# Up projection of a gated MLP: two parts of x moved as 512 columns through one weight load, their products added by ScalarE and VectorE

## The chip, the cores and the metric

One NeuronCore of a Trainium2 chip. The metric is the device time of one execution in microseconds, the median of several runs. Engines are named as in the profile: PE (TensorE, with PEld for its weight loads), DVE (VectorE), ACT (ScalarE), POOL (GpSimd) and SP (SyncE, which issues the loads here).

## The reference

One layer of a decoder trunk on x of 256 rows and 1024 columns, float32. A combined input projection feeds attention, a short convolution and a pooling mixer; an output projection, a residual and a LayerNorm follow. The gated MLP is the part that the change touches:

```python
up = causal_dwconv(x @ w_up, ffn_conv_w) + ffn_conv_b   # w_up: 1024 x 5632, width-3 conv over rows
u, g = jnp.split(up, 2, axis=-1)                        # 2816 columns each
ff = (u * jax.nn.silu(g)) @ w_down                      # w_down: 2816 x 1024
return layer_norm(DEEPNORM_ALPHA * x + ff, ln2_g, ln2_b)
```

## The kernel before

Float32 products are made on TensorE from operands of type float32r. Each operand is split into two such parts whose sum it is: `split` (L120) has ACT round the tile to the first part, `hi` (L121), and DVE subtract that from the tile, which is the second part, `lo` (L122). Three products of the four are kept: `mm3` (L148, its matmul is L150) issues first part by first part, first weight part by second x part, and second weight part by first x part, into one PSUM sum. The parts of x are held in two tiles, `xh` and `xl`, as [128, 8 row tiles of the model dimension, 256 rows of x]. In the MLP the weight part is the operand that is loaded and x is the one that is moved: every matmul of the up projection has 128x128 weights and 256 columns.

Weights come from memory in loads of 128x2048 (SP, `load`, L94, five held), and are split by halves, called units, of 128x1024 (`wsplit`, L128, nine held). For the up projection a unit is one column tile of 128 output columns: `("u", j)` for the value half and `("g", j)` for the gate half, j from 0 to 21. A unit `("d", k)` is one row tile of w_down.

The work of one column tile j is:

- `up_mm(j, 0)` and `up_mm(j, 1)` (L437): 8 row tiles by 3 matmuls each. Both halves of a tile share one PSUM bank, `u_ps[j]`, 256 columns each. Tile 0 is made by `up_first` from unsplit operands and is not touched by the change.
- `taps(j, s)` (L457): the convolution over rows. ACT writes y = scale * src + bias from PSUM (L462), then DVE adds the two shifted products with multiply-adds (L463, L464), which read PSUM and y.
- `gate_silu(j)` (L466, ACT, L468) and `gate_out(j)` (L470): DVE multiplies the halves into f (L472), and f is split into mh (ACT, L121) and ml (DVE, L122).
- `down(k, t, p)` (L477): the down projection of row tile k, five column tiles later (LAG = 5), for two groups of 128 rows of x (t) and the pieces p of 512, 512 and 512, 256, 256 output columns. Its sums, `acc2`, take five of the eight PSUM banks from the first down block on. For the last seven row tiles (KEEP = 7) the second group's products come at the very end.

The order is written out by hand, and the program keeps it: every engine runs its instructions in the order in which they are emitted. The work is a list of blocks of matmuls: u of tile j, g of tile j, and from tile 5 on the down block of row tile j - 5. The loop at L638 emits a block's matmuls, then what follows the block before it (the taps), then the weight splits for blocks up to six ahead, then the gate of a finished tile. So from tile 6 on DVE's queue for a tile is: ml of the last tile, lo of a split, L463 and L464 of the value half, lo, L463 and L464 of the gate half, lo, f. ACT's is: mh, hi, y, hi, y, hi, silu. Tiles 1 to 5 have two splits in their time instead of three. PSUM banks come from a pool of eight, small tiles (y, silu, f) from a pool of 12 slots (`tmp`, L68).

The end of the kernel is `resid` and `ln2_out`: residual, LayerNorm and the store.

Of the kernel before, what the change touches and what calls it, by code (L numbers as in the profile page):

```python
# [17 lines left out]
P = 128  # L18
# [10 lines left out]
ALPHA = 2.0 ** 0.25  # L29
EPS = 1e-5  # L30
NEG = -1e30
H = 1024                # columns of a unit of weights, half of a load
RB = 5                  # loads held
WB = 9                  # split units held
AHEAD = (4, 7)          # blocks of matmuls that the splits may run ahead, before and from w_out on
LAG = 5                 # column tiles between the up and the down projection
KEEP = 7                # row tiles of w_down that the second token tile takes last
FIRST = 2               # row tiles of w_out that both token tiles take first
WARM = 23
# output columns of each token tile by the bank they are summed in: (first, number)  # L40
PIECES = (((0, 512), (512, 512)), ((0, 512), (512, 256), (768, 256)))

C_ID = 0
# [12 lines left out]
def trunk(ctx, tc, a_qk, a_v, a_cp, a_out, a_up, a_down, x, par, tab, lnp, out):  # L56
# [8 lines left out]
    def bank():  # L65
        return ps.tile([P, 512], F32, name="bank")

    def tmp(name):  # L68
        return wk.tile([P, S], F32, name=name, tag="t", bufs=12)

    # ---- weights: loaded in the order of use, and split by halves into two float32r parts
    # whose sum they are
    units = [("qk", k) for k in range(KD)]
    units += [(n, i) for n, c in (("v", 4), ("cp", KD), ("out", KD)) for i in range(c)]
    for j in range(NJ):
# [16 lines left out]
    raws, left = [], {}  # L92

    def load():  # L94
        # as far as the slots are free
        while len(raws) < len(loads) and (len(raws) < RB or not left[raws[len(raws) - RB]]):
            at, c = loads[len(raws)]
            key = id(at), c
            n = S + H if at is a_qk else 2 * H
            raw = raw_of[key] = rp.tile([P, n], F32, name="raw")  # L100
            if raws:
                nc.sync.dma_start(raw, at[c])
            else:
                nc.sync.dma_start(raw[:, :2 * S], at[c][:, :2 * S])
                nc.sync.dma_start(raw[:, 2 * S:], at[c][:, 2 * S:])
            raws.append(key)
            left[key] = 1 if at is a_qk else 2
# [43 lines left out]
                             skip_group_check=skip)  # L151

    tb = cp.tile([NB + 1, GW + NH], F32, name="tb")
    xh = cp.tile([P, KD, S], F32R, name="xh")
    xl = cp.tile([P, KD, S], F32R, name="xl")
    # the tensor engine's clock rises with use: some products of zeros while the first loads run
    zero = cp.tile([P, P], BF16, name="zero")
    nc.vector.memset(zero, 0.0)
    g_ps = warm = bank()
# [6 lines left out]
    attn = ExitStack()  # L166
    ap = attn.enter_context(tc.tile_pool(name="ap", bufs=1))

    # ---- relative bias, times 8, as bias[q reversed, k] for the second token tile
    bias = ap.tile([P, NH, S], F32, name="bias")  # L170

    def bias_mm():
# [8 lines left out]
            bias, bass.AP(tensor=g_dr.tensor, offset=g_dr.offset, ap=[[1, P], [GW, NH], [1, S]]))  # L181
        nc.gpsimd.dma_start(prm, par)

    # ---- q, k: one sweep over the model dimension, eight column tiles at once
    qk_ps = [bank() for _ in range(4)]

    def qk_block(k):
        h, l = W.pop(("qk", k))
        for c in range(8):
            ws = slice(c * P, (c + 1) * P)  # L190
            if k == 0 and c < 2:
                # the first two column tiles come before their splits
                raw = raw_of[id(a_qk), 0]
                nc.tensor.matmul(qk_ps[0][:, c * S:(c + 1) * S], raw[:, S + c * P:S + (c + 1) * P],  # L194
                                 raw[:, :S], start=c == 0, stop=False, skip_group_check=True)
                continue
            mm3(qk_ps[c // 2][:, (c % 2) * S:(c % 2 + 1) * S], h[:, ws], l[:, ws],
                xh[:, k, :], xl[:, k, :], k == 0 and c % 2 == 0, k == KD - 1, skip=True)
# [11 lines left out]
    s_ps, prs = {}, {}  # L210

    def scores(j):
        # two heads on the two halves of the rows, side by side
        pair = [(h, slice((h % 2) * DH, (h % 2 + 1) * DH)) for h in (2 * j, 2 * j + 1)]
        for h, _ in pair:
            s_ps[h] = bank()
        for h, r in pair:
            nc.tensor.matmul(s_ps[h][:, :P], qT[r, j, 0], kT[r, j, :P], start=True, stop=True)
        for h, r in pair:
            nc.tensor.matmul(s_ps[h][:, P:P + S], qT[r, j, 1], kT[r, j], start=True, stop=True)  # L220
# [43 lines left out]
        nc.vector.tensor_copy(hi, rev)  # L264
        nc.vector.tensor_sub(ml[:, j].rearrange("p (t q) -> p t q", t=NT), rev, hi.bitcast(F32))

    # ---- v
    v = ap.tile([P, NT, 512], F32, name="v")
    v_ps = []

# [12 lines left out]
        for t in range(NT):  # L283
            nc.scalar.activation(v[:, t], v_ps[t], AF.Copy)

    # ---- pool and conv columns: P0 P1 | CC0 CX0 | CB0 CC1 | CX1 CB1
    cps = {}

    def cp_block(i):
# [8 lines left out]

    def pool_sums(t, p_ps):
        p_ps = p_ps[:, :S]  # L300
        # window sums by doubling; the two halves of the partitions have their own windows
        p, a, b, d = tmp("pin"), tmp("pa"), tmp("pb"), tmp("pd")
        nc.scalar.activation(p, p_ps, AF.Copy)

        def step(dst, src, w, rows):
            nc.gpsimd.tensor_add(dst[rows, w:], src[rows, w:], src[rows, :S - w])
            nc.gpsimd.tensor_copy(dst[rows, :w], src[rows, :w])

        al, up = slice(0, P), slice(DH, P)
        step(a, p, 1, al)  # L310
        if t == 0:
            step(b, a, 2, up)
        else:
            step(b, a, 2, al)
            step(a, b, 4, al)
            step(b, a, 8, up)
        iw = prm[:, C_IW + t:C_IW + t + 1]
        ed = prm[:, C_ED + 16 * t:C_ED + 16 * t + 16]
        for rows, src in ((slice(0, DH), a), (up, b)):
            nc.gpsimd.tensor_mul(d[rows, :16], src[rows, :16], ed[rows])  # L320
            nc.gpsimd.tensor_scalar(d[rows, 16:], src[rows, 16:], iw[rows], None, op0=ALU.mult)
        nc.gpsimd.tensor_sub(d, d, p)
        return d
# [22 lines left out]
        nc.vector.tensor_mul(o, cb_ps[:, :S], y)  # L346
        to_mix(4 + t, o)

    # ---- residual stream and LayerNorm
    def ln_rows(i):  # L350
        t = fp.tile([P, 2, D], F32, name="lnp")
        for r in range(2):
# [2 lines left out]
        gb.append(t)  # L355

    def resid(t, c, n, acc):
        # alpha * x + acc of n columns from c on, and their statistics
        nc.vector.scalar_tensor_tensor(xr[:, t, c:c + n], xr[:, t, c:c + n], ALPHA, acc,
                                       op0=ALU.mult, op1=ALU.add)  # L360
        for q in range(c // S, (c + n) // S):
            nc.vector.bn_stats(stats[t][:, q], xr[:, t, q * S:(q + 1) * S])  # L362

    def norm_stats(t):
        # mean, variance, 1 / deviation
        mv = wk.tile([P, 3], F32, name="mv")
        nc.vector.bn_aggr(mv[:, :2], stats[t])
        nc.vector.tensor_scalar(mv[:, 2:], mv[:, 1:2], EPS, None, op0=ALU.add)  # L368
        nc.gpsimd.tensor_tensor(mv[:, 2:], mv[:, 2:], half, op=ALU.pow)  # L369
        return mv  # L370

    # ---- output projection; row tiles in the order 0 1 2 3 6 7 4 5
    order = (0, 1, 2, 3, 6, 7, 4, 5)
    acc = [[], []]

# [35 lines left out]
            nc.tensor.transpose(t_ps[t, hf][:, i * P:(i + 1) * P], xr[:, t, k * P:(k + 1) * P], ident)  # L411

    def ln1_cols(t, hf):
        # gain and offset on the transposed rows
        ts = slice(t * P, (t + 1) * P)
        for i in range(4):
            k = 4 * hf + i
# [12 lines left out]
        nc.gpsimd.tensor_mul(xr[:, t], xr[:, t], gb[0][:, 0])  # L430
        nc.gpsimd.tensor_add(xr[:, t], xr[:, t], gb[0][:, 1])

    # ---- gated MLP
    acc2 = [[], []]
    gt = {}

    def up_mm(j, s):  # L437
        h, l = W.pop(("ug"[s], j))
        if s == 0:
            u_ps[j] = bank()  # L440
        for k in range(KD):
            ws = slice(k * P, (k + 1) * P)
            mm3(u_ps[j][:, s * S:(s + 1) * S], h[:, ws], l[:, ws], xh[:, k], xl[:, k], k == 0, k == KD - 1)

    def up_first(t, steps):
        # the first two column tiles from the unsplit operands, one token tile at a time
        if 0 not in u_ps:
            u_ps[0] = bank()
        for n, (k, s) in steps:
# [7 lines left out]
    def taps(j, s):  # L457
        c = s * NJ + j
        w = [prm[:, C_FW + 3 * c + i:C_FW + 3 * c + i + 1] for i in range(3)]
        src = u_ps[j][:, s * S:(s + 1) * S]  # L460
        y = ys[j, s] = tmp(f"y{s}")
        nc.scalar.activation(y, src, AF.Identity, scale=w[2], bias=prm[:, C_FB + c:C_FB + c + 1])  # L462
        nc.vector.scalar_tensor_tensor(y[:, 1:], src[:, :S - 1], w[1], y[:, 1:], op0=ALU.mult, op1=ALU.add)  # L463
# [42 lines left out]
                                           op0=ALU.mult, op1=ALU.add)  # L506
            (nc.scalar if i % 2 else nc.sync).dma_start(out[t * P:(t + 1) * P, cs], xr[:, t, cs])

    # ---- the order of work: blocks of matmuls, the units they need, and what follows each,
    # before and after the splits of that step. What follows is emitted after the next block's  # L510
    # matmuls, or with now before them; hold keeps a block's units for that many blocks more;
    # without more, no splits come in
    blocks = []

    def block(pe, need=(), a=(), b=(), now=False, hold=0, more=True):
        blocks.append((pe, list(need), list(a), list(b), now, hold, more))

    L = lambda f, *r: (lambda: f(*r))  # noqa: E731

    def seq(*fs):  # L520
        def run():
            for f in fs:
                f()
        return run
# [32 lines left out]

    fp = xr = xf = None
    gb = []
    cpb = lambda i, *pre: (seq(*pre, L(cp_block, i)), [("cp", i)])  # noqa: E731  # L560
    block(*cpb(0, sc[3]), [L(pool_go, 0)] + sm[3], nm[2])
    block(*cpb(1), [L(pool_go, 1)], nm[3])
    block(*cpb(2))
# [48 lines left out]
        block(seq(*(L(down, k, 1, p) for k in range(NJ - KEEP, NJ))), (), [L(rs2, 1, p)], now=True)  # L612
    blocks[-1][2].append(L(ln2_out, 1))

    # splits run as far ahead as AHEAD, their slots and the loads allow: a slot is free after the
    # last block with its unit
    free = {}
    for i, blk in enumerate(blocks):
        for u in blk[1]:
# [32 lines left out]


def _buckets():
    """For each column m of the table, the bucket of distance 255 - m (NB: masked)."""
    dist = 255 - np.arange(GW)
    n = np.maximum(dist, 1).astype(np.float32)
    e = NB // 2
# [66 lines left out]
```

## Time and profile before

| | |
|---|---|
| time of 3 runs, median (lowest to highest) | 296.45 us (295.04 to 296.99) |
| profiled execution, span from first to last instruction | 293.4 us |
| its own time | not given beside the span; the median lies 3.05 us above the span |
| mean granted TensorE clock, as a share of full | 0.993 |
| gated MLP, from the first matmul of tile 1 to the last matmul | 105.5 to 285.6 us |

Times in the rows are from the start of the span. A timeline row begins with start and duration in us; in square brackets stands how long the engine was idle before it and what it waited for. A matmul's own duration overlaps the next one's, so the pace of matmuls is read from their starts.

### The profile page before, as it was taken

The page shows a single profiled execution, that of the slowest core. Times are in us where ns is not written, and L with a number is a line of the kernel's source. Part 1 is how long each engine was busy: PE and PEld are TensorE (multiplying, and loading weights), DVE is VectorE, ACT ScalarE, POOL GpSimd, SP SyncE. Part 2 cuts the span into 40 slices and gives each one's busy share as a digit, 9 for nine tenths or more (in the row PEclk, how much of TensorE's full clock was granted, in tenths as well). Part 3 has the DMA queues.
Part 4 walks back from the last instruction along what each step waited for, and adds up shares of the span by engine and source line. Part 5 has one row for each costly group of instructions (what it writes and reads, how often), then busy time and mean ns, then how long its engine had stood idle before and what let it go on. Part 6 is the DMA issues. An engine that isn't in the chain of part 4 may idle for free.

```text
span 293.4 us, 5137 instructions
## 1 busy us (share of the span) xinstructions
PE 284.3 (97%) x2085; PEld 264.3 (90%) x2085; DVE 222.3 (76%) x384; ACT 157.9 (54%) x261; POOL 41.0 (14%) x43
## 2 busy tenths in 40 slices
PE   8999999999999999999999999999999999999990
PEld 7899669988888999999999999999999999999880
DVE  2975575797938699998988888887667867768565
ACT  4863646847412384466766666665555665655100
POOL 1020004850000289800000000000000000000011
PEclk9999999999999999999999999999999999999997
DMA  7999942135980269174747474746473552100011
GB/s 279 414 401 408 405 153 90 65 136 176 382 300 1 61 231 398 60 280 141 268 145 286 146 295 147 287 153 268 143 287 144 183 232 83 78 0 2 0 73 72
DMA packets 9367, 56.28 MB, mean 192 GB/s; under 512 B 1069, under 2 KB 1333, under 8 KB 3712
## 3 DMA queue, kind: packets, MB, share of 16 engines
q1 hardware_dynamic: 7920, 50.99, 46.0%
q0 software_dynamic: 1136, 4.58, 4.2%
q10 hardware_dynamic: 288, 0.39, 0.4%
q8 instruction: 16, 0.26, 0.4%
q14 instruction: 7, 0.06, 0.1%
HBM read 54.89 MB, written 1.06 MB: 191 GB/s over the span
## 4 chain that ended last, share of the span: by engine, by line
PE 69%; DVE 18%; ACT 5%; issue 5%; POOL 1%; POOLq 0%; DVEq 0%
PE bank L150 65%; DVE lo L122 7%; ACT hi L121 2%; DVE pr L241 2%; ACT pr L233 2%; DVE f L472 1%; PE bank L161 1%; DVE xf L423 1%; DVE y L463 1%; DVE ml L122 1%; DVE xl L122 1%; DVE lg L230 1%; DVE y L464 1%; DVE stat L362 1%; PE bank L194 1%
## 5 line engine op out<-in xcount | busy, mean ns | idle before, releaser
L122 DVE TENSOR_TENSOR lo<-raw,hi 128x1024 fp32r<-128x1024 f32 (+2 forms) x95 | 113.8, 1210 | 23.4 <-ACT hi L121 23.2
L150 PE MATMUL bank<-xh,hi 128*128 128x256 f32 x462 | 130.6, 283 | 0.1
L150 PE MATMUL bank<-xh,lo 128*128 128x256 f32 x462 | 129.6, 281 | 0.0
L150 PE MATMUL bank<-xl,hi 128*128 128x256 f32 x462 | 129.0, 279 | 0.0
L121 ACT ACTIVATE hi<-raw 128x1024 fp32r<-128x1024 f32 (+2 forms) x95 | 95.4, 1018 | 4.0 <-DMA raw<-a_v 3.1
L150 PEld LDWEIGHTS bank<-xh,hi 128*128 128x128 f32 x462 | 87.2, 189 | 2.0 <-ACT hi L121 1.1
L150 PEld LDWEIGHTS bank<-xl,hi 128*128 128x128 f32 x462 | 87.1, 189 | 0.1
L150 PEld LDWEIGHTS bank<-xh,lo 128*128 128x128 f32 x462 | 86.9, 188 | 0.0
L150 PE MATMUL bank<-hi,mh 128*128 128x512 f32 (+1 forms) x150 | 52.4, 349 | 0.0
L150 PE MATMUL bank<-hi,ml 128*128 128x512 f32 (+1 forms) x150 | 52.1, 348 | 0.0
L150 PE MATMUL bank<-lo,mh 128*128 128x512 f32 (+1 forms) x150 | 52.1, 347 | 0.0
L462 ACT ACTIVATE y<-bank,prm 128x256 f32<-128x256 f32 x44 | 24.7, 561 | 27.4 <-PE bank L150 15.8
L150 PEld LDWEIGHTS bank<-hi,ml 128*128 128x128 f32 x150 | 28.3, 189 | 3.8
L150 PEld LDWEIGHTS bank<-lo,mh 128*128 128x128 f32 x150 | 28.4, 189 | 3.6
L150 PEld LDWEIGHTS bank<-hi,mh 128*128 128x128 f32 x150 | 28.3, 189 | 3.6
L369 POOL TENSOR_TENSOR mv<-mv,half 128x1 f32<-128x1 f32 x4 | 3.1, 775 | 188.3 <-DVE mv L368 188.3
L463 DVE SCALAR_TENSOR_TENSOR y<-bank,prm,y 128x255 f32<-128x255 f32 x44 | 21.0, 478 | 10.5 <-ACT y L462 10.3
L464 DVE SCALAR_TENSOR_TENSOR y<-bank,prm,y 128x254 f32<-128x254 f32 x44 | 21.2, 482 | 1.6
L121 ACT ACTIVATE mh<-f 128x256 fp32r<-128x256 f32 x22 | 9.2, 418 | 24.3 <-DVE f L472 24.3
L122 DVE TENSOR_TENSOR ml<-f,mh 128x256 fp32r<-128x256 f32 x22 | 11.0, 500 | 10.6 <-ACT mh L121 10.6
L468 ACT ACTIVATE sg<-y 128x256 f32<-128x256 f32 x22 | 9.2, 419 | 13.8 <-DVE y L464 13.8
L430 POOL TENSOR_TENSOR xr<-xr,lnp 128x1024 f32<-128x1024 f32 x2 | 13.3, 6634 | 3.3 <-DMA lnp<-lnp 3.3
(91 smaller groups left out, 201.4 us busy)
## 6 DMA issues: line engine op xcount, KB each, us to landing
raw<-a_up SPq DMA_DIRECT2D x22, 1024.0 KB, 4.9
raw<-a_down SPq DMA_DIRECT2D x11, 1024.0 KB, 5.8
raw<-a_qk SPq DMA_DIRECT2D x7, 640.0 KB, 6.3
raw<-a_cp SPq DMA_DIRECT2D x4, 1024.0 KB, 13.1
raw<-a_out SPq DMA_DIRECT2D x4, 1024.0 KB, 4.8
raw<-a_v SPq DMA_DIRECT2D x2, 1024.0 KB, 7.8
lnp<-lnp POOLq DMA_DIRECT2D x4, 512.0 KB, 4.7
bias<-g_dr POOLq DMA_DIRECT2D x1, 1024.0 KB, 12.6
```

What stands on the lines that cost most here:

```text
L121: nc.scalar.activation(hi, raw, AF.Copy)
L122: nc.vector.tensor_sub(lo, raw, hi.bitcast(F32))
L150: nc.tensor.matmul(o, l, r, start=start and i == 0, stop=stop and i == 2, skip_group_check=skip)
L161: nc.tensor.matmul(warm[:, :P], zero, zero, start=True, stop=True)
L233: nc.scalar.activation(pr[:, a:b], lg[:, a:b], AF.Exp, bias=st[:, t:t + 1], scale=-1.0, accum_out=st[:, 2 + t:3 + t])
L241: nc.vector.tensor_scalar(pr[:, a:b], pr[:, a:b], st[:, 4 + t:5 + t], None, op0=ALU.mult)
L369: nc.gpsimd.tensor_tensor(mv[:, 2:], mv[:, 2:], half, op=ALU.pow)
L430: nc.gpsimd.tensor_mul(xr[:, t], xr[:, t], gb[0][:, 0])
L462: nc.scalar.activation(y, src, AF.Identity, scale=w[2], bias=prm[:, C_FB + c:C_FB + c + 1])
L463: nc.vector.scalar_tensor_tensor(y[:, 1:], src[:, :S - 1], w[1], y[:, 1:], op0=ALU.mult, op1=ALU.add)
L464: nc.vector.scalar_tensor_tensor(y[:, 2:], src[:, :S - 2], w[0], y[:, 2:], op0=ALU.mult, op1=ALU.add)
L468: nc.scalar.activation(ys[j, 2], ys.pop((j, 1)), AF.Silu)
```

## The change

`xh` and `xl` become two views of one tile `xp`, in which the 256 columns of the second part stand behind those of the first for each row tile. In the up projection of tiles 1 to 21 the first weight part is loaded once and 512 columns of x, both parts, are moved through it; the second weight part takes 256 columns as before. Each half of a tile has a whole PSUM bank: its first 256 columns hold the sum of two products, its last 256 the product of the first weight part and the second x part. `taps` copies the latter to SBUF (ACT) and adds it to the former (DVE); the taps then read that sum in SBUF. The pool of small tiles has 16 slots. The other edits are comments.

```diff
     def tmp(name):
-        return wk.tile([P, S], F32, name=name, tag="t", bufs=12)
+        return wk.tile([P, S], F32, name=name, tag="t", bufs=16)
...
-    xh = cp.tile([P, KD, S], F32R, name="xh")
-    xl = cp.tile([P, KD, S], F32R, name="xl")
+    xp = cp.tile([P, KD, 2, S], F32R, name="xp")
+    xh, xl = xp[:, :, 0], xp[:, :, 1]
...
     def up_mm(j, s):
         h, l = W.pop(("ug"[s], j))
-        if s == 0:
-            u_ps[j] = bank()
+        o = u_ps[j, s] = bank()
         for k in range(KD):
             ws = slice(k * P, (k + 1) * P)
-            mm3(u_ps[j][:, s * S:(s + 1) * S], h[:, ws], l[:, ws], xh[:, k], xl[:, k], k == 0, k == KD - 1)
+            nc.tensor.matmul(o, h[:, ws], xp[:, k], start=k == 0, stop=False, skip_group_check=True)
+            nc.tensor.matmul(o[:, :S], l[:, ws], xp[:, k, 0], start=False, stop=k == KD - 1,
+                             skip_group_check=True)
...
     def taps(j, s):
         c = s * NJ + j
         w = [prm[:, C_FW + 3 * c + i:C_FW + 3 * c + i + 1] for i in range(3)]
-        src = u_ps[j][:, s * S:(s + 1) * S]
+        if j == 0:
+            src = u_ps[0][:, s * S:(s + 1) * S]
+        else:
+            o = u_ps.pop((j, s))
+            e, src = tmp("e"), tmp("v")
+            nc.scalar.activation(e, o[:, S:], AF.Copy)
+            nc.vector.tensor_add(src, o[:, :S], e)
         y = ys[j, s] = tmp(f"y{s}")
```

## Rows read from the trace of the kernel before

**Rows 1.** The page, busy time, share of the span and instructions of each engine.
```profile
PE 284.3 (97%) x2085; PEld 264.3 (90%) x2085; DVE 222.3 (76%) x384; ACT 157.9 (54%) x261; POOL 41.0 (14%) x43
```

**Rows 2.** The chain that ended last: start us, duration us, what.
```profile
136.01 0.49 DVE y L464
...
136.64 138.63 PE bank L150 x1017
```

**Rows 3.** Timeline of ACT: the rounding of the gate, tiles 1, 2, 19, 20, 21.
```profile
127.01 0.42 ACT L121 ACTIVATE mh<-f 128x256 fp32r<-128x256 f32 x1 [0.99 <-DVE f L472]
...
132.50 0.42 ACT L121 ACTIVATE mh<-f 128x256 fp32r<-128x256 f32 x1 [0.99 <-DVE f L472]
...
257.50 0.42 ACT L121 ACTIVATE mh<-f 128x256 fp32r<-128x256 f32 x1 [0.99 <-DVE f L472]
...
265.94 0.42 ACT L121 ACTIVATE mh<-f 128x256 fp32r<-128x256 f32 x1 [0.99 <-DVE f L472]
...
272.53 0.42 ACT L121 ACTIVATE mh<-f 128x256 fp32r<-128x256 f32 x1 [0.49 <-DVE f L472]
```

**Rows 4.** Timeline of ACT through tile 9.
```profile
170.22 0.42 ACT L121 ACTIVATE mh<-f 128x256 fp32r<-128x256 f32 x1 [0.99 <-DVE f L472]
170.54 1.04 ACT L121 ACTIVATE hi<-raw 128x1024 fp32r<-128x1024 f32 x1
171.49 0.55 ACT L462 ACTIVATE y<-bank,prm 128x256 f32<-128x256 f32 x1
171.94 1.05 ACT L121 ACTIVATE hi<-raw 128x1024 fp32r<-128x1024 f32 x1
...
177.30 0.42 ACT L121 ACTIVATE mh<-f 128x256 fp32r<-128x256 f32 x1 [0.99 <-DVE f L472]
```

**Rows 5.** Timeline of DVE through the same tile.
```profile
170.67 0.42 DVE L122 TENSOR_TENSOR ml<-f,mh 128x256 fp32r<-128x256 f32 x1 [0.48 <-ACT mh L121]
171.62 1.22 DVE L122 TENSOR_TENSOR lo<-raw,hi 128x1024 fp32r<-128x1024 f32 x1 [0.53 <-ACT hi L121]
172.76 0.47 DVE L463 SCALAR_TENSOR_TENSOR y<-bank,prm,y 128x255 f32<-128x255 f32 x1
...
173.67 1.21 DVE L122 TENSOR_TENSOR lo<-raw,hi 128x1024 fp32r<-128x1024 f32 x1
...
176.85 0.42 DVE L472 TENSOR_TENSOR f<-y,sg 128x256 f32<-128x256 f32 x1
```

**Rows 6.** Timeline of PE: a down block begins, changes width, and an up block begins.
```profile
176.09 0.40 PE L150 MATMUL bank<-hi,mh 128*128 128x512 f32 x1
...
178.17 0.28 PE L150 MATMUL bank<-hi,mh 128*128 128x256 f32 x1
...
178.88 0.28 PE L150 MATMUL bank<-xh,hi 128*128 128x256 f32 x1
```

**Rows 7.** Groups of instructions by line and shape: busy us, mean ns of one.
```profile
L462 ACT ACTIVATE y<-bank,prm 128x256 f32<-128x256 f32 x44 | 24.7, 561 | 27.4 <-PE bank L150 15.8 <-DVE y L464 10.2
...
L121 ACT ACTIVATE mh<-f 128x256 fp32r<-128x256 f32 x22 | 9.2, 418 | 24.3 <-DVE f L472 24.3
...
L337 DVE TENSOR_TENSOR cz<-bank,cx 128x256 f32<-128x256 f32 x2 | 0.8, 416 | 0.0
...
L336 ACT ACTIVATE cx<-bank 128x256 f32<-128x256 f32 x2 | 0.8, 376 | 1.2 <-PE bank L150 1.2
```

**Rows 8.** Waits: engine line waited for: us in total, times, longest us.
```profile
ACT y L462 <- DVE y L464: 10.2, 10, 3.2
```

**Rows 9.** Timeline of PE: the last matmul.
```profile
285.44 0.28 PE L150 MATMUL bank<-hi,ml 128*128 128x256 f32 x1
```

**Rows 10.** Busy time by stretch (PE, PEld, DVE, ACT, POOL; granted clock, DMA share, GB/s).
```profile
289.00:290.00 1.00, 0.00 (x0) 0.00 (x0) 1.00 (x3) 0.00 (x0) 0.00 (x0) 0.75 0.13 53
```

**Rows 11.** Timeline of PE at the start of the kernel.
```profile
5.62 0.42 PE L150 MATMUL bank<-xl,hi 128*128 128x256 f32 x1
5.84 0.44 PE L150 MATMUL bank<-xh,lo 128*128 128x256 f32 x1
```

## The prediction, made before the changed kernel was seen

> **What bounds the kernel now.** I read the page's engine table first, then the chain that ended last, then the timelines of PE, DVE and ACT in the gated MLP. In the table [rows 1] PE is busy for 97% of the span and DVE for 76%, so at first sight the change works on the right engine. The chain [rows 2] corrects this: its last long piece is PE alone, from 136.64 us for 138.63 us, but that piece starts where a DVE instruction of tile 3 (L464) ends. PE wanted a PSUM bank that DVE still read. Before that point the chain lies on DVE. So DVE and ACT set the pace up to 137 us, PE sets the end.
>
> How close the two are is read from one instruction per column tile, the ACT rounding of the gated product (mh<-f, L121). Late in the stage it recurs every 265.94 - 257.50 = 8.44 us [rows 3]: that is PE's need. From tile 6 on, as long as DVE is behind, it recurs every 177.30 - 170.22 = 7.08 us [rows 4], and tiles 2 to 5, with two weight splits each and no down projection, take 132.50 - 127.01 = 5.49 us [rows 3]. The DVE timeline of such a tile has no gap but the two that ACT causes behind L121 [rows 5]: this 7.08 is a closed loop of DVE and ACT, instruction behind instruction. If only this loop counted, tile 21 would reach its mh at 127.01 + 4 x 5.49 + 15 x 7.08 + 6.59 = 261.8 us (6.59 is the last tile, 272.53 - 265.94, with two splits). It does at 272.53, because PE holds it. The loop has 10.8 us to spare over the whole stage, 1.4 us in a late tile.
>
> **PE: what the change removes.** Per row tile of the model dimension three matmuls of 256 columns become one of 512 and one of 256, and three weight loads become two. A 512-column matmul with its load is followed by the next after (178.17 - 176.09) / 9 = 0.231 us, a 256-column one after (178.88 - 178.17) / 6 = 0.118 us [rows 6]. Time goes by columns, with 0.005 us per instruction; the loads are already hidden. Columns stay 768, so the gain is 2 x 0.118 - 0.231 = 0.005 us, 336 times: 1.7 us, or 0.08 per tile. PE's need becomes 8.36 us.
>
> **DVE and ACT: what it adds.** 42 times (tiles 1 to 21, two halves) ACT copies the second 256 columns out of PSUM (e), DVE adds them to the first (v), and ACT's y reads v. Prices: e is like cx<-bank, 0.376 us; the add reads one PSUM and one SBUF operand like cz<-bank,cx, 0.416; y is 0.561 from PSUM today, and a plain ACT instruction of this shape from SBUF (mh<-f, 0.418) is 0.042 dearer than from PSUM (0.376), so 0.60 [rows 7]. The two DVE multiply-adds that follow (L463, L464) read v from SBUF; I leave their 0.91 us (172.76 to the next lo at 173.67 [rows 5]).
>
> What matters is the order. Both queues run as emitted: ACT has e, y, then the next split's hi; DVE has add, L463, L464, then that split's lo. Today y is done before DVE asks for it. Now y cannot start before the add ends, and L463, behind the add on DVE, cannot start before y ends; everything else of DVE, the splits that PE needs too, is queued behind L463. A handover costs 0.03 us (mh at 170.22 for 0.42, ml at 170.67 [rows 4, 5]). So DVE spends, per half, add 0.42 + 0.03 + y 0.60 + 0.03 = 1.08 us more before L463. Behind it nothing is won back: ACT's hi starts 0.45 after y [rows 4], takes 1.05 and hands over, which is y's start + 1.53, while DVE comes free at y's start + 0.63 + 0.91 = 1.54. The copy e costs nothing: ACT issues it while DVE is still in the split before (1.14 us from lo to L463 [rows 5]); if DVE were ahead of ACT it would add 0.41.
>
> Bounds per half: y between 0.42 (the plain SBUF instruction) and 0.66 (a tenth over my price), and the add between 0.42 and 0.52 (a quarter over the row, if it meets GpSimd's work), give 0.90 to 1.24, or 38 to 52 us in all. I take 1.08, as these rows are for the same shapes: 42 x 1.08 = 45.4.
>
> The loop becomes 7.08 + 2.16 = 9.24 us per tile against 8.36 for PE, and 5.49 + 2.16 = 7.65 for tiles 2 to 5. DVE and ACT now set the pace to the end. Tile 21's mh comes at 261.8 + 45.4 = 307.2 us, 34.6 later than now.
>
> **Banks.** Each half takes a bank of its own. Five of the eight go to the down projection's sums at its first block, so PE may run three halves ahead of DVE; that block's last sum must wait for the add of (4, u), at about 127.01 + 2.16 + 2 x 7.65 + 1.33 = 145.8 us, so PE stands, in pieces, from about 134 (today the block's 9 x 0.231 + 6 x 0.118 = 2.8 us end at 136.64). It costs the loop nothing: half (6, u) is needed near 161 (tile 5's mh, 127.01 + 2.16 + 4 x 7.65 = 159.8, and some 1.3), and PE, let on by the add of (4, g) 3.1 us after 145.8, has it by 152. Later PE waits some 0.9 us per tile.
>
> There is a rule that speaks for the change. ACT's y waits for DVE's L464 ten times, 10.2 us together [rows 8]: the gate half may not be read by ACT while DVE reads the other half of that bank. The Trainium skill, PSUM — Partial Sum Buffer, section "PSUM bank collisions raise a hardware error", says that two engines may not access one bank in the same partitions together, reads included; the trace agrees in that the wait is there. By that rule the separate banks take the wait away and the second rival below gains; by the rows, DVE has no gap before L463 in a paced tile [rows 5], so it was ACT that waited and the loop wins nothing.
>
> **The rest.** 16 temporaries instead of 12: a tile now takes eight instead of four, so a slot returns after two tiles, later than any of its reads; nothing. The merged xp keeps rows contiguous; if the four writes of its halves after the first LayerNorm had to follow one another, three more handovers of some 0.7 us would stand there, 2 us; I take 0. SP's loads follow the splits, which come later, with the same five in flight; nothing.
>
> **The end.** After tile 21's ml (mh + 0.87) PE still has 6 + 21 matmuls of 512 and 42 of 256 columns: 27 x 0.231 + 42 x 0.118 = 11.2 us, to 319.3. From the last matmul's start plus 0.12 (285.56 [rows 9]) to the end of the span are 7.8 us: 327.1. Before these 11.2 us PE has waited some 5 us, and in the trace the granted clock falls between 289 and 290, about 4 us after the last matmul [rows 10]. So they may start at the lower level, 1.2 GHz. Ends: 0, and 11.2 if all ran at half rate. The nearest row is the start of the kernel, where 256-column matmuls still followed each other after 0.22 us, near twice 0.118, at 5.6 us [rows 11]; 4 to 5 us at half rate lose 2. I take 2: a span of 329.1.
>
> The page gives the profiled execution a span of 293.4 and no time of its own; the median of the three runs, 296.45, is 3.05 above it, and I keep that: **332.1 us**, taken as 332, or 12% slower.
>
> **The rivals.**
>
> *PE stays the bound (not slower).* Halves in banks of their own let DVE start a half one block earlier, and if the loop's extra stays below (8.36 - 7.08) / 2 = 0.64 us per half and PE meets no bank wait, only PE's saving is left: 296.45 - 1.7 = 294.8. For it: PE is 97% busy, and the wait in [rows 8]. Against it: add and y alone are 1.02.
>
> *Only the add counts.* If y hid behind other DVE work, the loop would be 7.08 + 0.84 = 7.92, below 8.36, yet PE would stand at the first down block until about 127.01 + 0.84 + 2 x 6.33 + 1.33 = 141.8 instead of going on at 136.64. From there its work is 148.9 - 1.3: the span grows by about 4, time 301. Against it: the queue order leaves DVE nothing to do between the add and L463.
>
> *Worse.* PE falls to 1.2 GHz in its waits and cannot keep up, 16.7 us per tile while that lasts, or the tail runs wholly at half rate (+9): 341 and up. For it: the waits at 134 to 146 us. Against it: a PE that is late has no idle time and its clock should return.
>
> **How the numbers follow.** Forecast 0.79, PE-bound 0.05, only the add 0.08, worse 0.08. The bounds of the terms, 0.90 to 1.24 per half and the tail's 0 to 11, move the sum from about 322 to 348; I put the range from 318 to 346, leaving out the two fast rivals and part of the worse one. About 1% is what a measurement of this kernel can tell from no change: faster 0.02, same 0.05 (nearly all the PE-bound case), slower 0.93.
>
> **What would show it.** Right: mh<-f recurs every 9.2 us from tile 6 to 20 and 7.65 before; DVE waits for ACT's y before L463 in all 42 halves, some 0.66 us each, 28 us in all; PE waits for banks and not for splits; the last slices show a granted clock below full. PE's step is right if a 512-column matmul is followed after 0.231 us. Wrong: tiles 8.4 us apart (PE-bound), 7.9 (only the add), or a PE at 1.2 GHz over whole tiles.

## The result and the profile after

The changed kernel takes 333.22 us (median of 4 runs, 332.24 to 333.83), the kernel before 295.75 (median of 4 runs, the three of the table above and one more). The ratio estimated from all the runs is 1.125, 95% interval 1.120 to 1.129; the two medians alone give 1.127. The forecast was 332, range 318 to 346. The profiled execution has a span of 331.9 us and a time of 333.66.

The engine table of the page, as in [rows 1]:

```profile
PE 295.8 (89%) x1749; PEld 254.3 (77%) x1749; DVE 240.0 (72%) x426; ACT 172.0 (52%) x303; POOL 41.0 (12%) x43
```

PE has 336 matmuls fewer, yet its busy time has grown by 11.5 us (in part because a matmul that waits, or runs at the lower clock, has a longer record: the rows under "The tail" have 0.80 us and 0.63 for a 512-column matmul that has 0.39 otherwise). DVE gained 42 instructions and 18 us and is busy for a smaller share than before. No engine in this table looks like the bound. The chain does show it; this is its part for tile 21, all of it DVE and ACT handing work to each other (start us, duration us, what):

```profile
301.21 0.96 ACT hi L121
302.17 0.02 issue
302.19 1.23 DVE lo L122
303.42 0.34 DVE v L470
303.76 0.03 issue
303.79 0.61 ACT y L472
304.40 0.03 issue
304.43 0.49 DVE y L473
304.92 0.03 issue
304.94 0.48 DVE y L474
305.43 1.17 DVE lo L122
```

Read it as a loop: split (lo), add (v), over to ACT for y, back to DVE for the two multiply-adds, next split. In [rows 2] the last 139 us before the end stage were one piece of PE; that piece is gone.

The timeline of ACT gives the pace, as in [rows 3]; the rows are tiles 1, 2, 19, 20 and 21:

```profile
130.10 0.42 ACT L121 ACTIVATE mh<-f 128x256 fp32r<-128x256 f32 x1 [1.03 <-DVE f L482]
...
137.70 0.42 ACT L121 ACTIVATE mh<-f 128x256 fp32r<-128x256 f32 x1 [1.03 <-DVE f L482]
...
291.44 0.42 ACT L121 ACTIVATE mh<-f 128x256 fp32r<-128x256 f32 x1 [1.03 <-DVE f L482]
...
300.79 0.42 ACT L121 ACTIVATE mh<-f 128x256 fp32r<-128x256 f32 x1 [1.02 <-DVE f L482]
...
309.61 0.42 ACT L121 ACTIVATE mh<-f 128x256 fp32r<-128x256 f32 x1 [0.49 <-DVE f L482]
```

A tile now takes 300.79 - 291.44 = 9.35 us late in the stage, where it took 8.44, and 7.60 early, where it took 5.49. Every period from tile 6 to 20 lies between 9.35 and 9.36: it no longer matters what PE does.

The waits (in total us, times, longest) name both sides:

```profile
ACT y L472 <- DVE v L470: 54.8, 42, 2.2
...
DVE y L473 <- ACT y L472: 28.8, 43, 0.7
...
PEld bank L445 <- DVE v L470: 18.9, 15, 2.5
PE bank L445 <- DVE v L470: 14.2, 15, 2.2
```

DVE stands 0.67 us before L473 in each of the 42 halves: 28 us of idle that no busy share shows (the 43rd wait is one of tile 0, which the change leaves as it was). PE waits for the add too, because the add is what frees its bank.

### The profile page after: what moved, and what is told of

It reads as the page before. It is cut to its first block, busy times and chain, and to the rows that moved or that the text cites. A ratio compares the mean times of both kernels' runs of the same rounds, so it can differ in the third digit from the quotient of the medians.

```text
span 331.9 us, 4551 instructions
## 1 busy us (share of the span) xinstructions
PE 295.8 (89%) x1749; PEld 254.3 (77%) x1749; DVE 240.0 (72%) x426; ACT 172.0 (52%) x303; POOL 41.0 (12%) x43
## 3 DMA queue, kind: packets, MB, share of 16 engines
HBM read 54.89 MB, written 1.06 MB: 169 GB/s over the span
## 4 chain that ended last, share of the span: by engine, by line
DVE 49%; ACT 23%; PE 17%; issue 6%; DMA 2%; POOL 1%; POOLq 0%; SPq 0%; DVEq 0%; ACTq 0%
DVE lo L122 25%; PE bank L150 16%; ACT hi L121 10%; ACT y L472 8%; DVE y L473 4%; DVE y L474 4%; DVE v L470 4%; DVE f L482 3%; ACT mh L121 3%; DMA raw<-a_qk 2%; ACT pr L234 2%; DVE pr L242 2%; DVE ml L122 1%; DVE xf L424 1%; DVE xp L122 1%
## 5 line engine op out<-in xcount | busy, mean ns | idle before, releaser
L445 PE MATMUL bank<-xp,hi 128*128 128x512 f32 x336 | 124.1, 407 | 14.6 <-DVE v L470 14.2
L446 PE MATMUL bank<-xp,lo 128*128 128x256 f32 x336 | 96.7, 288 | 1.3 <-DVE lo L122 1.2
L445 PEld LDWEIGHTS bank<-xp,hi 128*128 128x128 f32 x336 | 65.1, 194 | 32.6 <-DVE v L470 18.9
L446 PEld LDWEIGHTS bank<-xp,lo 128*128 128x128 f32 x336 | 65.5, 195 | 2.3 <-DVE lo L122 2.3
L150 PE MATMUL bank<-hi,mh 128*128 128x512 f32 (+1 forms) x150 | 54.2, 362 | 9.9 <-DVE v L470 5.6
L472 ACT ACTIVATE y<-v,prm 128x256 f32<-128x256 f32 x42 | 25.3, 602 | 54.8 <-DVE v L470 54.8
L150 PE MATMUL bank<-lo,mh 128*128 128x512 f32 (+1 forms) x150 | 53.5, 357 | 0.1
L150 PE MATMUL bank<-xp,hi 128*128 128x256 f32 x252 | 45.7, 284 | 1.1 <-ACT hi L121 1.1
L150 PEld LDWEIGHTS bank<-xp,hi 128*128 128x128 f32 x252 | 38.7, 189 | 2.6 <-ACT hi L121 1.8
L473 DVE SCALAR_TENSOR_TENSOR y<-v,prm,y 128x255 f32<-128x255 f32 x42 | 20.3, 484 | 28.2 <-ACT y L472 28.2
L150 PE MATMUL bank<-xp,lo 128*128 128x256 f32 x126 | 35.3, 280 | 0.2 <-DVE lo L122 0.2
L150 PEld LDWEIGHTS bank<-xp,lo 128*128 128x128 f32 x126 | 23.7, 188 | 0.4 <-DVE lo L122 0.4
L474 DVE SCALAR_TENSOR_TENSOR y<-v,prm,y 128x254 f32<-128x254 f32 x42 | 20.3, 483 | 1.5
```

The costliest lines, as they stand in the source:

```text
L150: nc.tensor.matmul(o, l, r, start=start and i == 0, stop=stop and i == 2, skip_group_check=skip)
L445: nc.tensor.matmul(o, h[:, ws], xp[:, k], start=k == 0, stop=False, skip_group_check=True)
L446: nc.tensor.matmul(o[:, :S], l[:, ws], xp[:, k, 0], start=False, stop=k == KD - 1, skip_group_check=True)
L474: nc.vector.scalar_tensor_tensor(y[:, 2:], src[:, :S - 2], w[0], y[:, 2:], op0=ALU.mult, op1=ALU.add)
```

## The experiments

Three theories were put against each other. L: the time is a longer loop of DVE and ACT, made of the add and of y's wait. W: only the busy time of the added work counts, not the wait. B: PE loses the time, by the bank that each half takes or by the 512-column form.

| run | time, us | kernel before beside it | ratio, 95% interval | loop or period per late tile |
|---|---|---|---|---|
| changed kernel | 333.22 | 295.75 | 1.125, 1.120 to 1.129 | 9.35 |
| PE part alone | 301.24 | 296.13 | 1.017, 1.013 to 1.020 | 8.32 |
| add alone | 333.57 | 296.13 | 1.129, 1.122 to 1.136 | 9.35 |
| y does not wait | 307.20 | 296.13 | 1.036, 1.032 to 1.040 | 8.01 |
| wait alone | 319.36 | 296.13 | 1.078, 1.073 to 1.083 | 8.76 |
| add ahead of split | 303.89 | 296.46 | 1.025, 1.022 to 1.029 | 7.69, then 8.32 |
| banks alone | 303.47 | 296.46 | 1.025, 1.021 to 1.029 | 8.45 |
| new form from tile 13 | 295.49 | 296.46 | 0.997, 0.994 to 0.999 | 8.32 |

### The PE part alone

```diff
             o = u_ps.pop((j, s))
-            e, src = tmp("e"), tmp("v")
-            nc.scalar.activation(e, o[:, S:], AF.Copy)
-            nc.vector.tensor_add(src, o[:, :S], e)
+            src = o[:, :S]
```

> The PE part alone: 512 columns per first weight part and a bank for each half stay, the copy e and the add are taken out, and the taps read the first 256 columns of the bank in PSUM as before (so the product of the first weight part and the second x part is left out of the result). Theory L (the time comes from the add and from y waiting for it in the loop of VectorE and ScalarE): the loop is back at 7.08 us per tile, PE at 8.35 to 8.37, so nearly all of the 37 us go. What is left is the halved lead of PE: it can begin half (6,u) only when the taps of (4,g) are read, at about 142 us as the trace of before has it, against 136.64, less 1.3 us of PE's saving behind that: about +4, so 299 to 300. Theory B (the separate banks and the 512-column form cost the time): 325 to 333. If neither banks nor waits matter: 294.

Measured 301.24. Without the copy and the add 32.0 of the 37.5 us are gone, so B falls as the main cause. But the PE part is not the gain that it was meant to be: it is slower than the kernel before by 5 us. The timeline of PE in this run shows where (three matmuls that waited):

```profile
136.64 0.36 PE L150 MATMUL bank<-hi,mh 128*128 128x256 f32 x1 [1.11 <-DVE y L472]
...
140.04 0.55 PE L150 MATMUL bank<-hi,mh 128*128 128x256 f32 x1 [2.81 <-DVE y L472]
...
142.12 0.77 PE L445 MATMUL bank<-xp,hi 128*128 128x512 f32 x1 [1.10 <-DVE y L472]
```

They stand at the first down block, whose sums take five banks, and at the first half after it, (6,u). In [rows 2] this half began at 136.64, here at 142.12, 5.5 us later. The stretch behind the waits has a low clock (busy us of PE, PEld, DVE, ACT, POOL; then granted clock, DMA share, GB/s):

```profile
140.00:150.00 10.00, 8.86 (x38) 7.56 (x38) 8.74 (x14) 6.30 (x11) 0.00 (x0) 0.70 0.66 257
```

A mean of 0.70 over 10 us is 6 us at 1.2 GHz, but until 142.12 PE was held by its waits all the same. What the clock cost is read from the pace of PE behind the last wait (starts of the 512-column matmul of successive row tiles, first at the lower clock, then at the full one):

```profile
142.90 0.63 PE L445 MATMUL bank<-xp,hi 128*128 128x512 f32 x1
...
143.54 0.63 PE L445 MATMUL bank<-xp,hi 128*128 128x512 f32 x1
...
146.06 0.39 PE L445 MATMUL bank<-xp,hi 128*128 128x512 f32 x1
...
146.41 0.40 PE L445 MATMUL bank<-xp,hi 128*128 128x512 f32 x1
```

A row tile takes 0.64 us instead of 0.35. The six row tiles from 142.12 to 146.06 took 3.9 us instead of 2.1, so the clock cost 1.8 to 1.9. Against this PE saves 0.12 us per tile. Its period is now 244.40 - 236.08 = 8.32 us, by the timeline of ACT, where it was 8.44:

```profile
236.08 0.42 ACT L121 ACTIVATE mh<-f 128x256 fp32r<-128x256 f32 x1 [1.03 <-DVE f L480]
...
244.40 0.42 ACT L121 ACTIVATE mh<-f 128x256 fp32r<-128x256 f32 x1 [1.03 <-DVE f L480]
```

From (6,u) on PE waits no more, so the saving counts in sixteen tiles, 1.9 us: 5.5 + 1.9 - 1.9 = 5.5, and the span grew by 5.4 (298.8 against 293.4). L had expected 299 to 300; the low clock is what it left out. The run also keeps the merged `xp` and the 16 slots, and its early periods are back at 5.49 and 7.08 us, so neither of these two costs the loop anything.

### The added work alone

```diff
         src = u_ps[j][:, s * S:(s + 1) * S]
+        if j > 0:
+            e, v_ = tmp("e"), tmp("v")
+            nc.scalar.activation(e, src, AF.Copy)
+            nc.vector.tensor_add(v_, src, e)
+            src = v_
```

(in the kernel before, with 16 small slots)

> The added work alone, in the kernel before: three matmuls of 256 columns and one bank per tile as before; ScalarE copies each half out of PSUM, VectorE adds the copy to the half, and y and the taps read the sum (so the half counts twice in the result). Theory L: the loop of VectorE and ScalarE is that of the changed kernel, 9.35 us per tile from tile 6 on, 7.6 before; 331 to 335. Theory B: near the kernel before, 295 to 300. Theory W (only the busy time of the add counts): 297 to 302.

Measured 333.57, the time of the changed kernel with PE's old matmuls and shared banks. The waits of this run are those of the changed kernel to the tenth of a microsecond:

```profile
ACT y L467 <- DVE v L464: 54.8, 42, 2.2
...
DVE y L468 <- ACT y L467: 28.8, 43, 0.7
```

So the copy and the add are enough for the whole loss, and what PE does is hidden behind them. W and B, which put this run at 297 to 302 and 295 to 300, fall.

### The add without the wait

```diff
             e, src = tmp("e"), tmp("v")
             nc.scalar.activation(e, o[:, S:], AF.Copy)
+        y = ys[j, s] = tmp(f"y{s}")
+        nc.scalar.activation(y, src if j == 0 else o[:, :S], AF.Identity, scale=w[2],
+                             bias=prm[:, C_FB + c:C_FB + c + 1])
+        if j > 0:
             nc.vector.tensor_add(src, o[:, :S], e)
-        y = ys[j, s] = tmp(f"y{s}")
-        nc.scalar.activation(y, src, AF.Identity, scale=w[2], bias=prm[:, C_FB + c:C_FB + c + 1])
```

(y goes ahead of the add and no longer reads its sum)

> The changed kernel with all its instructions, but y reads the first 256 columns of the bank in PSUM and is issued before the add, so it no longer waits for the add (the second product is left out of the centre tap; the other two taps read the sum). Theory L: VectorE keeps the add, 0.34 to 0.42 us per half, and loses the 0.67 us wait; the loop is 7.8 to 7.9 us per tile, below PE's 8.36, so PE sets the pace again from the point where it gets its banks, about 143 us instead of 136.64: 300 to 303. Theory W: nothing changes by it, 331 to 335. Theory B: 331 to 335, as banks and matmuls are those of the changed kernel.

Measured 307.20: W and B, which wanted 331 or more, fall. All of the added instructions are still there, 26 us of the loss are not. The timeline of DVE through the first half of a tile:

```profile
204.35 0.43 DVE L122 TENSOR_TENSOR ml<-f,mh 128x256 fp32r<-128x256 f32 x1 [0.48 <-ACT mh L121]
205.30 1.23 DVE L122 TENSOR_TENSOR lo<-raw,hi 128x1024 fp32r<-128x1024 f32 x1 [0.52 <-ACT hi L121]
206.44 0.42 DVE L474 TENSOR_TENSOR v<-bank,e 128x256 f32<-128x256 f32 x1
206.90 0.48 DVE L475 SCALAR_TENSOR_TENSOR y<-v,prm,y 128x255 f32<-128x255 f32 x1
207.41 0.48 DVE L476 SCALAR_TENSOR_TENSOR y<-v,prm,y 128x254 f32<-128x254 f32 x1
207.81 1.22 DVE L122 TENSOR_TENSOR lo<-raw,hi 128x1024 fp32r<-128x1024 f32 x1
```

There is no gap before L475: the add costs 206.90 - 206.44 = 0.46 us and nothing else. The timeline of ACT gives the loop, 211.91 - 203.90 = 8.01 us instead of the 7.8 to 7.9 expected:

```profile
203.90 0.42 ACT L121 ACTIVATE mh<-f 128x256 fp32r<-128x256 f32 x1 [0.99 <-DVE f L484]
...
211.91 0.42 ACT L121 ACTIVATE mh<-f 128x256 fp32r<-128x256 f32 x1 [0.99 <-DVE f L484]
```

The time was 4 us above what L expected. From the start of (6,u) on the chain is PE alone until 285 us, in the tail, so the loop counts only by when that half began: at 146.68 instead of 143. Of this, 1.3 us were lost before the changed part (tile 0's rounding stands at 121.30, in the kernel before at 120.04). The granted clock was 0.66 between 140 and 150 us, which I had not counted. And some 1 us lies outside the span: the four runs of this kernel took 2.5 to 3.1 us more than their spans, those of the kernel before 1.8. Why is not shown.

### The wait without the add

```diff
-            e, src = tmp("e"), tmp("v")
-            nc.scalar.activation(e, o[:, S:], AF.Copy)
-            nc.vector.tensor_add(src, o[:, :S], e)
+            src = o[:, :S]
         y = ys[j, s] = tmp(f"y{s}")
+        if j > 0:
+            nc.vector.memset(y[:, :1], 0.0)
         nc.scalar.activation(y, src, AF.Identity, scale=w[2], bias=prm[:, C_FB + c:C_FB + c + 1])
```

> The changed kernel without the copy and the add, but with y still waiting for VectorE: VectorE writes one column of y's tile, which y then overwrites (0.06 us of work instead of 0.42), and y reads the first 256 columns in PSUM (the second product is left out). Theory L: the wait of VectorE for y stays, so 0.06 + 0.04 + 0.56 + 0.04 = 0.70 us per half, a loop of 8.5 us per tile, a little over PE's 8.36; tile 21's rounding at 261.8 + 42 x 0.71 = 291.6 us, time 312 to 318. Theory W: 0.06 us per half is nothing, 297 to 301. Theory B: 299 to 303, or wherever the run of the PE part alone lies.

Measured 319.36, on L's side and 1.4 us over its range; W and B had 303 at most. With a DVE instruction of one column, once per half, the kernel takes 18 us more than without it (the PE part alone, 301.24). The timeline of DVE:

```profile
202.61 0.06 DVE L471 MEMSET y<- 128x1 f32 x1
203.36 0.48 DVE L473 SCALAR_TENSOR_TENSOR y<-bank,prm,y 128x255 f32<-128x255 f32 x1 [0.69 <-ACT y L472]
```

The wait is 0.69 us, that of the changed kernel. The loop was 8.76 us, not 8.5: from the write to L473 it is 0.75 instead of the 0.70 I had added up, and 0.09 more go at the two ends of that stretch. The two runs divide the cost of a half: add alone (8.01 - 7.08) / 2 = 0.46, wait 0.67 to 0.69, together the (9.35 - 7.08) / 2 = 1.14 of the changed kernel.

### The add ahead of a split

```diff
-            block(L(up_mm, j, 0), [("u", j)], [L(taps, j, 0)])
-            block(L(up_mm, j, 1), [("g", j)], [L(taps, j, 1)], gate)
+            block(L(up_mm, j, 0), [("u", j)], [L(pre, j, 0)], held + [L(taps, j, 0)])
+            block(L(up_mm, j, 1), [("g", j)], [L(pre, j, 1)], [L(taps, j, 1)])
+            held = gate
         if j >= LAG:
-            down_unit(j - LAG)
+            down_unit(j - LAG, held)
+            held = []
```

(`pre` holds the copy and the add; the second list of a block comes behind the splits)

> All of the change's work, in another order: the copy and the add of a half are issued ahead of a weight split, y and the taps behind it, and the gate of a tile one block later. While VectorE subtracts the split (1.22 us), ScalarE has time for y, so the wait for y should go although every instruction stays and nothing is left out of the result. Theory L: the loop falls from 9.35 to about 7.8 us per tile, under PE's 8.32; what stays is PE's wait for banks at the first down block (half (6,u) begins near 143 instead of 136.64) and its clock after it: 300 to 304. Theory W (the busy time counts): 331 to 335.

Measured 303.89. Every instruction of the change is still issued, and 29 of the 37.5 us go by their order alone. DVE through the first half of a tile:

```profile
204.10 0.42 DVE L468 TENSOR_TENSOR v<-bank,e 128x256 f32<-128x256 f32 x1
204.44 1.22 DVE L122 TENSOR_TENSOR lo<-raw,hi 128x1024 fp32r<-128x1024 f32 x1
205.57 0.48 DVE L479 SCALAR_TENSOR_TENSOR y<-v,prm,y 128x255 f32<-128x255 f32 x1
```

y is made while DVE subtracts the split, and L479 follows without a gap. The loop is 208.07 - 200.38 = 7.69 us, by the timeline of ACT:

```profile
200.38 0.42 ACT L121 ACTIVATE mh<-f 128x256 fp32r<-128x256 f32 x1 [1.00 <-DVE f L488]
...
208.07 0.42 ACT L121 ACTIVATE mh<-f 128x256 fp32r<-128x256 f32 x1 [0.99 <-DVE f L488]
```

What remains is PE's: it waited 2.13, 1.47 and 2.77 us for banks between 135 and 145 us.

### The banks alone

```diff
-        if s == 0:
-            u_ps[j] = bank()
+        o = u_ps[j, s] = bank()
...
-            mm3(u_ps[j][:, s * S:(s + 1) * S], h[:, ws], l[:, ws], xh[:, k], xl[:, k], k == 0, k == KD - 1)
+            mm3(o[:, :S], h[:, ws], l[:, ws], xh[:, k], xl[:, k], k == 0, k == KD - 1)
```

(in the kernel before; the taps read `o[:, :S]`)

> The kernel before with one edit: each half of a tile takes a PSUM bank of its own and uses 256 of its 512 columns; three matmuls of 256 columns, no copy and no add. If the 5 us that the PE part alone lost are the halved lead in banks, the same three waits of PE stand at 135 to 142 us here, with the granted clock low behind them, and PE's period stays at 8.44: the run of the PE part alone plus PE's saving (0.12 us in 20 tiles, 2.4 us): 302 to 305. If the 512-column form lost them: 295 to 298.

Measured 303.47: one bank per half, with nothing else changed, costs 7 us. The same waits stand in PE's timeline as in the run of the PE part, at 137.81, 141.22 and 143.29:

```profile
137.81 0.35 PE L150 MATMUL bank<-hi,mh 128*128 128x256 f32 x1 [0.83 <-DVE y L463]
...
141.22 0.55 PE L150 MATMUL bank<-hi,mh 128*128 128x256 f32 x1 [2.81 <-DVE y L463]
```

With one bank per tile PE could run three tiles ahead while DVE was behind; with one per half it can run one and a half. So the 512-column form is not what lost time in the PE part alone: it saved 2.2 us (303.47 - 301.24) against the same banks, or 1.9 when each run is taken against the kernel before beside it.

### The new form only where DVE keeps up

```diff
+LATE = 13
...
-        o = u_ps[j, s] = bank()
+        if j < LATE:
+            if s == 0:
+                u_ps[j] = bank()
+        else:
+            o = u_ps[j, s] = bank()
```

(below tile 13 the matmuls, taps and order of the kernel before; from tile 13 on those of the run with the add ahead of the split)

> The kernel before for tiles 0 to 12; from tile 13 on, where VectorE has caught up with PE in the trace of before, the change in the order of the run with the add ahead of the split. Theory L: loop of 7.8 us under PE's 8.32, the lead in banks no longer needed, so only PE's saving is left, 9 tiles by 0.12 us: 1.1 us faster than before, 294.5 to 296. If halved banks cost PE wherever they are used: 297 to 300.

Measured 295.49 against 296.46, a ratio of 0.997 with an interval from 0.994 to 0.999: about 1 us faster, as expected of nine tiles by 0.12 us. The interval only just leaves out 1, but the profile agrees: from tile 0's rounding to tile 21's are 151.6 us, in the kernel before 152.5. It is the only version that is not slower than the kernel before, and it shows the size of the prize in these nine tiles.

## Why the prediction was right

**What bounds.** The step that carried it was to read 7.08 us as a closed loop of DVE and ACT and 8.44 as PE's need, so that 1.36 us per late tile was all there was to spend. The run with the add alone shows that the added work on DVE and ACT uses this up and sets the time by itself: 333.57.

**The price of a half.** 1.08 us was forecast, (9.35 - 7.08) / 2 = 1.14 measured. The three prices taken from rows of the same shape held: the add 0.417 us against 0.416, y 0.602 against 0.60, the copy 0.362 against 0.376, each the mean of 42 instructions. The 0.06 are in the handovers (0.03 to 0.05 each, and 0.43 from L474 to the next lo against 0.40 before). In tiles 2 to 5 a half costs less, (7.60 - 5.49) / 2 = 1.06. Tile 21 reached mh at 309.61 against a forecast of 307.2. Of these 2.4 us the loop has 1.6: tile 0's rounding, ahead of all that the change touches, stood at 120.86 already, in the kernel before at 120.04. It lies between 119.6 and 121.6 in the profiles of all the kernels here, also where nothing ahead of it differs.

**The order, not the work.** This was argued from the queues and is now shown: the wait is some three fifths of a half's cost (0.67 of 1.14), and moving the add ahead of a split takes it away with every instruction left in place.

**PE.** The 0.005 us per row tile were too small: the period in the run of the PE part is 8.32 against 8.44, 0.12 per tile or 0.008 per row tile. The sign and the size against the loss were right: 2.5 us over 21 tiles instead of 1.7.

**The tail.** I took 2 us for a low clock. In the timeline of PE (the last matmul before the wait, the first two after it, and the return):

```profile
305.51 0.39 PE L150 MATMUL bank<-hi,ml 128*128 128x512 f32 x1
310.08 0.80 PE L150 MATMUL bank<-hi,mh 128*128 128x512 f32 x1 [4.18 <-ACT mh L121]
310.67 0.63 PE L150 MATMUL bank<-lo,mh 128*128 128x512 f32 x1
311.10 0.63 PE L150 MATMUL bank<-hi,ml 128*128 128x512 f32 x1
...
316.06 0.39 PE L150 MATMUL bank<-hi,ml 128*128 128x512 f32 x1
316.28 0.39 PE L150 MATMUL bank<-hi,mh 128*128 128x512 f32 x1
```

512-column matmuls follow each other after 0.43 us until 316 and after 0.23 then; 14 of them took 5.98 us instead of 3.2: 2.8 lost. They began 0.4 us earlier than forecast, at the end of mh and not of ml. The granted clock of the two stretches (columns as above):

```profile
310.00:316.00 6.00, 5.92 (x14) 4.67 (x15) 4.45 (x11) 0.02 (x1) 0.74 (x1) 0.51 0.00 0
316.00:324.00 8.00, 8.00 (x56) 7.44 (x55) 4.11 (x8) 0.00 (x0) 0.26 (x1) 1.00 0.17 66
```

**What lies around the span.** I kept 3.05 us; the profiled execution has 333.66 - 331.9 = 1.8. The 3.05 set the median of three runs against the span of a single execution; beside their own spans the runs of the kernel before have 1.7 to 1.8 too. The errors sum to little because they have both signs: +0.8 ahead of the loop, +1.6 for the loop, +0.8 for the clock and -0.4 for the start in the tail, -1.3 here, together +1.5 (333.66 is 1.6 above 332.1). That they cancel so far is luck; that none is above 1.6 is not.

**Banks.** "It costs the loop nothing" held for the changed kernel, where DVE and ACT set the pace anyway; the down block's last sum got its bank at 146.55 us, against 145.8 forecast, and (6,u) began at 149.73. It does not hold where they don't: the banks alone cost 7 us. So two of my rivals were priced too low. The PE-bound case was put at 294.8, on the condition that PE meets no bank wait; the PE part alone, without add and without wait, meets three and took 301.24. "Only the add counts" was put at 301 (its terms add up to 300), and the run that makes it so took 307.20. It let PE go on at the add of (4,u). In that run this add gave the down block its last bank, at 144.17, and (6,u) stood for the add of (4,g) until 146.68. Both left out the clock behind the bank waits. Neither would have moved the forecast.

**The rule on banks.** The Trainium skill (PSUM — Partial Sum Buffer, section "PSUM bank collisions raise a hardware error") says that two engines cannot access one bank in the same partitions at the same time, reads included; the ten waits of the kernel before are in line with it. The prediction drew from this a gain by separate banks for the PE-bound rival (it says "the second"; that rival is the first of its list). The run of the banks alone shows ACT's waits for the other half fall from ten, 10.2 us, to the one in tile 0, 3.2 us, while the early periods stay at 5.49 and 7.08: it was ACT that waited, and nothing was won, as the rows had said.

How much of the bank loss is the idle time and how much the clock was worked out from the pace of PE's matmuls at either clock, not tried by itself.

## What to carry to other kernels

Before work is moved from one engine to two others, find the loop in which those two already hand work to each other, and add the new instructions to it in queue order: an engine that is busy for 76% may have 10 us to spare in 290. A dependency that crosses to another engine and back between neighbours in a queue costs the partner's whole instruction; issue its first half ahead of independent work, and it costs its own duration at most (here the cost of a half fell from 1.14 us to (7.69 - 7.08) / 2 = 0.3, with an add of 0.42). A wider matmul that takes a whole PSUM bank, where two results shared one, also halves how far PE can run ahead.

## What the runs showed that I had not expected

The clock followed short waits more closely than I had thought. In the PE part alone PE waited 1.1, 2.8 and 1.1 us with short bursts between; the granted clock fell to 0.50 during the longest of them, soon after 139 us, and came back at 146. The loss by it, 1.9 us, is over a third of the waits themselves. In the changed kernel the same stretch stood at 0.59:

```profile
140.00:150.00 10.00, 2.29 (x7) 1.70 (x8) 7.75 (x14) 5.52 (x11) 0.00 (x0) 0.59 0.32 105
```

There it cost nothing: PE was ahead of the loop, whose periods stay at 7.60 and 9.35 through it.

A DVE write of one column, 0.06 us, on which ACT waits, costs 0.84 us in the loop, where the copy and the add of the change cost 1.14: most of the cost is the crossing, not the size of the instruction.
